# Two PSUM banks for the logits and three for the transposes, in place of three and two

## The chip, the cores and the metric

The kernel runs on one core of a Trainium2 chip. The metric is the time of one execution on the device in microseconds (us), as the median over runs; smaller is better. All inputs and results are float32.

## The reference

One layer of a hybrid decoder for 1040 positions (16 learned meta tokens and 1024 real ones) of width 1024. The input is RMS-normalised and multiplied by one wide matrix, whose columns feed two branches:

```python
u = _rmsnorm(h, norm_g)
proj = einsum('bld,de->ble', u, w_in)
q, k, v, f_logit, z_attn, gate_b, gate_c, xc, z_conv = split(proj, ...)
cum_logf = cumsum(log_sigmoid(f_logit + b_f))
# attention, 8 heads of 64: logit[t, s] = q_t.k_s / 8 + c[t] - c[s], s <= t
attn = softmax(logit) @ v
y_attn = group_rmsnorm(attn) * silu(z_attn)
# short convolution of width 3 over positions, 512 channels
y_conv = group_rmsnorm(gate_b * conv3(gate_c * xc)) * silu(z_conv)
out = rmsnorm(h + concat(y_attn, y_conv) @ w_out)
```

## The kernel before, in words

Every float32 product is made of three passes of a reduced type: each operand is split into a high and a low part, and high x high, high x low and low x high are added up in PSUM. So nearly all of the work is matmuls of TensorE.

The program has three stages. The first (to about 147 us of the profiled span, with its last projection blocks running up to the first logits at 165.8) makes the normaliser, the projections for q, k, v and the forget gates, and writes them to DRAM. The third (from about 489.5 us) is the output projection and the last norm. The second, in between, is where the change lies: it weaves the attention of eight heads with the remaining 20 blocks of the input projection (L167; their results are gate, convolution and SiLU inputs).

The attention of a head works on eight blocks of 128 queries. Blocks 4 to 7 form the half c=1, blocks 0 to 3 the half c=0. For each half:
- `s_step` (L604 to L621) makes the logits of one query block against one stretch of keys (144 to 456 columns, table SCH): two matmuls into a PSUM tile pn (L612, L613), on VectorE the maximum of each row (L616 with the causal mask on the block's last stretch, L619 on the others), on ScalarE the exponential into SBUF with the row sums (L620, two instructions in the profile: the exponential, and the read of the sums). The half c=1 has nine such steps in a head and c=0 has five, 112 in all.
- `s_end` (L623 to L643) joins the stretches: small operations on VectorE, GpSimd and ScalarE, then GpSimd multiplies every stretch of the probabilities by its factor (L642).
- `t_step` (L645 to L670) transposes the probabilities for one block of 128 keys: up to four transposes on TensorE into one PSUM tile pt (L660), a corner on VectorE for the diagonal (L664, L665), then ScalarE copies the high part out (L668) and VectorE subtracts it to get the low part pl (a helper at L117). There are 96 such tiles.
- `v_step` (L672 to L680) multiplies them with v into the PSUM tile po (L679), and `fold` reads po out.

PSUM has eight banks, and each of these tiles is one. In the second stage the pools divide them so: pj two (projection blocks and the group norms), psn three (the tiles pn), pst two (the tiles pt), pso one (po). A pool hands its banks out in turn; the first matmul into a tile waits until the last reader of the tile that had the bank before has ended. For pn this is the second of ScalarE's instructions at L620, for pt VectorE's subtraction.

What sets the order: on TensorE it is written out by hand. The steps of all heads are laid out by places (S_AT, T_AT, V_END, V_LAG) at L725 to L755; `weave` (L757 to L772) puts matmuls of the projection between them by a running account of work; and `pinned` (L108) keeps these TensorE instructions in program order. Logits of the next half run while the present half is transposed and multiplied. The order of VectorE, ScalarE and GpSimd isn't fixed by hand: a planner that walks the program with its own estimates of durations sets it when the kernel is built (L916). The DMA queue of SyncE loads the next head's q, k and v and the weight blocks.

After the second stage the pools psn, pst and pso are closed, and their six banks serve the output projection (five accumulators p, L783, and one for a norm, L784); `ring` (L844) opens seven cells, two of them in pj.

Of the kernel before, what the change touches and what calls it, by code (L numbers as in the profile page):

```python
# [14 lines left out]
PSUM = bass.MemoryType.PSUM  # L15
# [20 lines left out]
def hybrid_kernel(ctx, tc, hT, h, w_q, w_vf, w_m, w_o, gn, bf, cw, ga, gc, gf, out):  # L36
# [352 lines left out]
    own = ctx.enter_context(tc.tile_pool(name="own", bufs=1, reuse_waits="tile"))  # L389
    cp = ExitStack()  # L390
    pj = ctx.enter_context(tc.tile_pool(name="pj", bufs=2, space=PSUM, reuse_waits="tile"))
    psn = cp.enter_context(tc.tile_pool(name="psn", bufs=3, space=PSUM, reuse_waits="tile"))
    pst = cp.enter_context(tc.tile_pool(name="pst", bufs=2, space=PSUM, reuse_waits="tile"))
    pso = cp.enter_context(tc.tile_pool(name="pso", bufs=1, space=PSUM, reuse_waits="tile"))
    stk = ctx.enter_context(tc.tile_pool(name="stk", bufs=2, reuse_waits="tile"))
    pnp = cp.enter_context(tc.tile_pool(name="pnp", bufs=1, reuse_waits="tile"))
# [398 lines left out]
    def out_mm(n, es):  # L795
        t, c0, w = cells[n]
        tt, cs = slice(t * P, t * P + P), slice(c0, c0 + w)
        for e in es:
            for i, (a, b) in enumerate(((mhi[e], whi[e]), (mhi[e], wlo[e]), (mlo[e], whi[e]))):
                ins = nc.tensor.matmul(held[n][:, :w], a[:, tt], b[:, cs], start=(e == ORDER[0] and i == 0),  # L800
                                       stop=(e == ORDER[-1] and i == 2))
                if n < AHEAD:
                    pinned(ins)
        return ins.ins.name
# [42 lines left out]
    for i, e in enumerate(ORDER):  # L847
# [7 lines left out]
        for k, n in enumerate(ring):  # L855
            name = out_mm(n, [e])
# [63 lines left out]
```

## Time and profile before

| what | value |
|---|---|
| median of 3 runs | 587.3 us (586.95 to 587.99) |
| the profiled execution's own time | 588.21 us |
| its span, from the first to the last instruction | 585.9 us |
| TensorE matmuls / weight loads, busy | 574.7 us / 509.5 us |
| VectorE, ScalarE, GpSimd, busy | 376.1, 293.5, 135.5 us |
| first and last logit step (L612) | at 165.8 and 467.3 us |
| first and last transposes (L660) | at 182.2 and 482.2 us |

The engines are PE (TensorE's matmuls), PEld (its weight loads, which run beside the matmuls), DVE (VectorE), ACT (ScalarE), POOL (GpSimd) and SP (SyncE). Times in a timeline are microseconds from the start of the span; L612 is line 612 of the kernel. The ends of matmuls are modelled, and they overlap in the rows, so what tells of TensorE is when one starts and how long it sat idle. In brackets behind an instruction stands the idle time of its engine just before it and what ended it; "issue" there means that the profile shows nothing that it waited for.

### The profile page before, as it was taken

The page shows a single profiled execution, that of the slowest core. Times are in us where ns is not written, and L with a number is a line of the kernel's source. Part 1 is how long each engine was busy: PE and PEld are TensorE (multiplying, and loading weights), DVE is VectorE, ACT ScalarE, POOL GpSimd, SP SyncE. Part 2 cuts the span into 40 slices and gives each one's busy share as a digit, 9 for nine tenths or more (in the row PEclk, how much of TensorE's full clock was granted, in tenths as well). Part 3 has the DMA queues.
Part 4 walks back from the last instruction along what each step waited for, and adds up shares of the span by engine and source line. Part 5 has one row for each costly group of instructions (what it writes and reads, how often), then busy time and mean ns, then how long its engine had stood idle before and what let it go on. Part 6 is the DMA issues. An engine that isn't in the chain of part 4 may idle for free.

```text
span 585.9 us, 9143 instructions
## 1 busy us (share of the span) xinstructions
PE 574.7 (98%) x3230; PEld 509.5 (87%) x3230; DVE 376.1 (64%) x850; ACT 293.5 (50%) x679; POOL 135.5 (23%) x280
## 2 busy tenths in 40 slices
PE   9999999999999999999989999999999999999995
PEld 6889999999998889988879988888998878888884
DVE  5515852133377676897776897786788778747342
ACT  5355431131055575566763665756656568715231
POOL 1102011121105344144053153440540420000000
PEclk9999999999999999999999999999999999999999
DMA  8764594239417614416126126142251046643201
GB/s 295 220 208 143 190 361 136 80 114 293 148 36 186 146 37 134 124 58 153 49 77 146 58 74 164 63 121 75 80 212 37 4 160 227 240 162 131 86 36 72
DMA packets 35222, 78.14 MB, mean 133 GB/s; under 512 B 4025, under 2 KB 13385, under 8 KB 35177
## 3 DMA queue, kind: packets, MB, share of 16 engines
q1 hardware_dynamic: 35032, 77.57, 42.8%
q8 instruction: 25, 0.41, 0.3%
q14 instruction: 21, 0.16, 0.1%
q10 hardware_dynamic: 144, 0.00, 0.0%
HBM read 55.92 MB, written 21.64 MB: 132 GB/s over the span
## 4 chain that ended last, share of the span: by engine, by line
PE 50%; DVE 3%; POOL 2%; issue 0%; ACT 0%; POOLq 0%; ACTq 0%
PE pj L167 22%; PE p L800 10%; PE pj L800 5%; PE po L679 4%; PE pt L660 4%; PE pn L612 2%; PE pn L613 2%; POOL pn L642 1%; PE pj L414 0%; PE pj L415 0%; DVE gy L419 0%; DVE pn L616 0%; DVE pl L117 0%; DVE gy L418 0%; DVE wmlo L117 0%
## 5 line engine op out<-in xcount | busy, mean ns | idle before, releaser
L167 PE MATMUL pj<-xhi,wmhi 128*128 128x512 f32 (+1 forms) x384 | 144.8, 377 | 0.1
L167 PE MATMUL pj<-xhi,wmlo 128*128 128x512 f32 (+1 forms) x384 | 137.2, 357 | 0.0
L167 PE MATMUL pj<-xlo,wmhi 128*128 128x512 f32 (+1 forms) x384 | 136.7, 356 | 0.0
L167 PEld LDWEIGHTS pj<-xhi,wmlo 128*128 128x128 f32 x384 | 72.1, 188 | 8.3
L167 PEld LDWEIGHTS pj<-xhi,wmhi 128*128 128x128 f32 x384 | 72.6, 189 | 5.1 <-DVE cx L453 0.8
L167 PEld LDWEIGHTS pj<-xlo,wmhi 128*128 128x128 f32 x384 | 72.8, 190 | 3.8
L620 ACT ACTIVATE pn<-pn,nmx 128x328 f32<-128x328 f32 (+6 forms) x112 | 60.6, 542 | 30.7 <-DVE nmx L616 20.8
L642 POOL TENSOR_SCALAR pn<-pn,fc 128x328 f32<-128x328 f32 (+4 forms) x112 | 69.0, 637 | 1.6
L668 ACT CAST ph<-pt 128x512 fp32r<-128x512 f32 (+1 forms) x96 | 46.9, 490 | 39.7 <-DVE pt L665 16.4
L117 DVE TENSOR_TENSOR pl<-pt,ph 128x512 fp32r<-128x512 f32 (+1 forms) x96 | 54.7, 571 | 15.1 <-ACT ph L668 13.4
L114 POOL TENSOR_SCALAR wmhi<-wm 128x1024 fp32r<-128x1024 f32 x24 | 25.8, 1074 | 153.9 <-PE pj L167 85.5
L660 PE MATMUL pt<-ident,pn 128*128 128x128 f32 x288 | 47.3, 273 | 2.8 <-POOL pn L642 1.6
L660 PEld LDWEIGHTS pt<-ident,pn 128*128 128x128 f32 x288 | 36.2, 140 | 12.6 <-POOL pn L642 3.5
L616 DVE CUSTOM_DVE_ANT_0 pn<-pn,maskn 128x328 f32<-128x328 f32 (+3 forms) x64 | 31.9, 500 | 11.9 <-PE pn L613 11.2
L117 DVE TENSOR_TENSOR wmlo<-wm,wmhi 128x1024 fp32r<-128x1024 f32 x24 | 29.3, 1221 | 11.3 <-POOL wmhi L114 11.2
L612 PE MATMUL pn<-k,q 128*128 128x328 f32 (+6 forms) x112 | 36.5, 327 | 0.0
L613 PE MATMUL pn<-k,q 66*128 66x328 f32 (+6 forms) x112 | 36.1, 323 | 0.0
L679 PE MATMUL po<-ph,v 128*128 128x512 f32 (+1 forms) x96 | 33.8, 353 | 0.0
L679 PE MATMUL po<-pl,v 128*128 128x512 f32 (+1 forms) x96 | 33.6, 353 | 0.0
L167 PE MATMUL ps<-xhi,wmhi 128*128 128x346 f32 (+1 forms) x96 | 30.9, 322 | 0.0
L167 PE MATMUL ps<-xlo,wmhi 128*128 128x346 f32 (+1 forms) x96 | 30.8, 321 | 0.0
L619 DVE TENSOR_REDUCE nmx<-pn 128x1 f32<-128x346 f32 (+4 forms) x48 | 25.0, 523 | 9.1 <-PE pn L613 8.9
(232 smaller groups left out, 1209.6 us busy)
## 6 DMA issues: line engine op xcount, KB each, us to landing
wm<-in_w_m SPq DMA_DIRECT2D x24, 512.0 KB, 4.1
k<-kd SPq DMA_DIRECT2D x24, 260.0 KB, 5.9
q<-qd SPq DMA_DIRECT2D x24, 256.0 KB, 5.2
vd<-vv SPq DMA_DIRECT2D x9, 512.0 KB, 2.9
v<-vd SPq DMA_DIRECT2D x8, 576.0 KB, 6.4
ht<-in_h SPq DMA_DIRECT2D x8, 512.0 KB, 6.4
yd<-gy SPq DMA_DIRECT2D x16, 256.0 KB, 2.0
q<-in_w_o SPq DMA_DIRECT2D x8, 512.0 KB, 4.8
```

Source lines behind the costliest of these rows:

```text
L114: nc.gpsimd.tensor_scalar(hi, src, 1.0, 1.0, ALU.mult, ALU.mult)
L117: nc.vector.tensor_tensor(lo, src, f(hi), ALU.subtract)
L167: ins = nc.tensor.matmul(ps[:, :w], wt[:, k, :], xt[:, t0:t0 + w], start=(k == 0 and n == 0), stop=(k == KT - 1 and n == 2))
L612: pinned(nc.tensor.matmul(ps[:, :w], q1[:, qs], k1[:, ks], start=True, stop=False))
L613: pinned(nc.tensor.matmul(ps[:, :w], q2[:DH + 2, qs], k2[:DH + 2, ks], start=False, stop=True))
L616: nc.vector.tensor_tensor_reduce(ps[:, :w], ps[:, :w], maskn[:, MASKW - w:], op0=ALU.add, op1=ALU.min, scale=-1.0, scalar=-NEG, accum_out= ...
L620: nc.scalar.activation(pn[j][:, ks], ps[:, :w], AF.Exp, bias=nmx[c][at], scale=-1.0 if last else 1.0, accum_out=smx[c][at])
L642: nc.gpsimd.tensor_scalar(pn[j][:, k0:k0 + w], pn[j][:, k0:k0 + w], fc[:, j % 4, i:i + 1], 1.0, ALU.mult, ALU.mult)
L660: pinned(nc.tensor.transpose(pt[:, q0:q0 + P], pn[j][:, ks], ident))
L668: nc.scalar.copy(ph[:, at:], pt[:, at:])
L679: pinned(nc.tensor.matmul(po[:, at:], v2[:, vk, :], t if vk == 8 else t[:, at:], start=(kt == 0 and i == 0), stop=(kt == 4 * c + 4 and i = ...
L800: ins = nc.tensor.matmul(held[n][:, :w], a[:, tt], b[:, cs], start=(e == ORDER[0] and i == 0), stop=(e == ORDER[-1] and i == 2))
```

## The change

One bank goes from the pool of the logit tiles pn to the pool of the transposed tiles pt. Nothing else is edited.

```diff
-    psn = cp.enter_context(tc.tile_pool(name="psn", bufs=3, space=PSUM, reuse_waits="tile"))
-    pst = cp.enter_context(tc.tile_pool(name="pst", bufs=2, space=PSUM, reuse_waits="tile"))
+    psn = cp.enter_context(tc.tile_pool(name="psn", bufs=2, space=PSUM, reuse_waits="tile"))
+    pst = cp.enter_context(tc.tile_pool(name="pst", bufs=3, space=PSUM, reuse_waits="tile"))
```

## Rows read from the trace of the kernel before

**Rows 1.** The page, parts 1 and 2: busy time by engine; granted clock in 40 slices.

```profile
PE 574.7 (98%) x3230; PEld 509.5 (87%) x3230; DVE 376.1 (64%) x850; ACT 293.5 (50%) x679; POOL 135.5 (23%) x280
PEclk9999999999999999999999999999999999999999
```

**Rows 2.** Who waited for whom, whole span: us in total, times, longest.

```profile
PEld pt L660 <- POOL pn L642: 3.5, 5, 2.0
...
PE pt L660 <- POOL pn L642: 1.6, 1, 1.6
...
PE pt L660 <- DVE pl L117: 0.9, 1, 0.9
```

**Rows 3.** Timeline, 441 to 445.2 us: start, us, engine and line; logit steps and reads.

```profile
441.76 0.34 PE L612 MATMUL pn<-k,q 128*128 128x392 f32 x1
...
442.30 0.19 ACT L620 ACTIVATION_READ_ACCUMULATOR pn<-pn,nmx 128x1 f32 x1
...
443.95 0.34 PE L612 MATMUL pn<-k,q 128*128 128x392 f32 x1
...
444.42 0.20 ACT L620 ACTIVATION_READ_ACCUMULATOR pn<-pn,nmx 128x1 f32 x1
...
445.00 0.37 PE L612 MATMUL pn<-k,q 128*128 128x456 f32 x1
```

**Rows 4.** The tile pn, whole span: count, ns least/median/most, first and last start.

```profile
L613 PE MATMUL pn<-k,q x112: 274/322/377, 166.0 to 467.4; 66*128 66x328 f32 x16, 66*128 66x392 f32 x16, 66*128 66x456 f32 x16, 66*128 66x346 f32 x16
L620 ACT ACTIVATE pn<-pn,nmx x112: 362/550/643, 166.9 to 469.2; 128x328 f32<-128x328 f32 x16, 128x392 f32<-128x392 f32 x16, 128x456 f32<-128x456 f32 x16, 128x346 f32<-128x346 f32 x16
L620 ACT ACTIVATION_READ_ACCUMULATOR pn<-pn,nmx x112: 189/193/217, 167.4 to 469.5; 128x1 f32 x112
...
L616 DVE CUSTOM_DVE_ANT_0 pn<-pn,maskn x64: 302/514/642, 167.2 to 468.3; 128x328 f32<-128x328 f32 x8, 128x392 f32<-128x392 f32 x8, 128x456 f32<-128x456 f32 x8, 128x348 f32<-128x348 f32 x8
L619 DVE TENSOR_REDUCE nmx<-pn x48: 417/513/633, 166.3 to 466.0; 128x1 f32<-128x346 f32 x16, 128x1 f32<-128x328 f32 x8, 128x1 f32<-128x392 f32 x8, 128x1 f32<-128x456 f32 x8
```

**Rows 5.** Busy us by stretch: PE, PEld, DVE, ACT, POOL, then granted clock, DMA share.

```profile
441.00:452.00 11.00, 11.00 (x58) 9.43 (x57) 9.23 (x24) 8.22 (x25) 0.00 (x0) 1.00 0.16 49
343.00:347.00 4.00, 2.95 (x21) 2.41 (x20) 3.87 (x11) 2.19 (x6) 0.45 (x1) 1.00 0.17 66
```

**Rows 6.** Timeline: loads of four transposed tiles, one tile's matmuls, and a read before them.

```profile
343.73 0.42 PEld L660 LDWEIGHTS pt<-ident,pn 128*128 128x128 f32 x4 [0.39 <-POOL pn L642]
...
345.40 0.69 DVE L117 TENSOR_TENSOR pl<-pt,ph 128x512 fp32r<-128x512 f32 x1
...
346.21 0.42 PEld L660 LDWEIGHTS pt<-ident,pn 128*128 128x128 f32 x4 [1.16 <-issue]
...
346.24 0.63 PE L660 MATMUL pt<-ident,pn 128*128 128x128 f32 x4 [0.90 <-DVE pl L117]
...
384.23 0.42 PEld L660 LDWEIGHTS pt<-ident,pn 128*128 128x128 f32 x4 [0.45 <-PE pj L167]
...
482.18 0.14 PEld L660 LDWEIGHTS pt<-ident,pn 128*128 128x128 f32 x1 [0.42 <-PE pj L414]
```

**Rows 7.** Timeline: the first and the last late pair of logit step and read.

```profile
169.52 0.37 PE L612 MATMUL pn<-k,q 128*128 128x456 f32 x1
169.57 0.19 ACT L620 ACTIVATION_READ_ACCUMULATOR pn<-pn,nmx 128x1 f32 x1
...
450.30 0.32 PE L612 MATMUL pn<-k,q 128*128 128x348 f32 x1
450.30 0.20 ACT L620 ACTIVATION_READ_ACCUMULATOR pn<-pn,nmx 128x1 f32 x1
```

**Rows 8.** The tile pt, its last reader; and the chain, first output matmuls (start, us).

```profile
L117 DVE TENSOR_TENSOR pl<-pt,ph x96: 296/633/692, 183.8 to 485.0; 128x512 fp32r<-128x512 f32 x48, 128x416 fp32r<-128x416 f32 x16, 128x288 fp32r<-128x288 f32 x16, 128x160 fp32r<-128x160 f32 x16
...
489.51 3.45 PE p L800 x15
```

## The prediction

> **What bounds the kernel.** I read the page's busy times first: TensorE is busy 98% of a 585.9 us span, VectorE 64%, ScalarE 50%, and the granted clock is at its upper level (2.4 GHz) in every slice [rows 1]. Busy time of TensorE overstates, since the matmuls overlap, so I then read what TensorE and its weight loads waited for. There is very little: in the whole span the matmuls wait 1.6 us once for GpSimd's normalising of the probabilities, 0.9 us once for VectorE's reading of a transposed tile, and the weight loads 3.5 us in five places for GpSimd [rows 2]. TensorE's order in the woven stage is written out by hand, and it takes its instructions strictly in that order; so any microsecond for which one of them waits for a bank is a microsecond on everything behind it, the projection's matmuls included, up to the output projection, which is TensorE's own work to the end. What counts is therefore only this: which matmuls have to wait for a bank before, and which after.
>
> What is *not* in the list of waits is the first finding: not one of the 112 logit steps (L612) waits for its bank with three banks. The closest is the step that starts at 445.00: the step three before it was read out at 444.42 + 0.20 = 444.62, 0.38 us earlier [rows 3].
>
> **How long a logit bank is held.** A bank is taken by the first matmul (L612) and given back when ScalarE's second instruction (the read of the row sums) ends. At its shortest that is about 0.15 us to the second matmul, then, by the medians, 0.32 for it, 0.51 for VectorE's maximum, 0.55 for the exponential and 0.19 for the read: 1.7 us [rows 4]. Taken step by step from the trace (end of the read minus start of L612) the shortest are 1.70 for 346 columns and 2.07 for 400; the median is 2.1 and the longest 4.3, because VectorE and ScalarE have other work in front. With two banks a step waits for the one two before it. The steps come in eight bursts of nine (query blocks 4 to 7 of a head), with five sparse ones between. In the last burst VectorE is busy 9.2 and ScalarE 8.2 of 11 us [rows 5], and nine steps start between 440.37 and 450.30, 1.24 us apart on average. Two spacings, 2.5 us, are about what a hold takes: enough on average, too short where two steps are put close together.
>
> **The cost of the bank taken away.** A wait before the matmuls of a full bank ends 0.15 us after the reader's end: the transposes at 346.24 follow a read that ended at 345.40 + 0.69 = 346.09 [rows 6]. So a step is late by (end of the read two steps before) + 0.15 - (its own start). In the last burst: the step at 441.76 needs the read that ends at 442.30 + 0.19 = 442.49, so it waits 0.88. The next, at 443.95, would be late by 444.62 + 0.15 - 443.95 = 0.82, but it has itself been moved 0.88 later by the first wait, so if the read keeps its time it no longer waits; nor does the one at 445.00 [rows 3]. Two more pairs, the first and the last in the kernel: the step at 169.52 needs the read that ends at 169.76, late by 0.39; that at 450.30 one that ends at 450.50, late by 0.35 [rows 7]. Over the 110 steps done this way 23 are late, the first and the last of them these two:
> - Added up as they stand, with every later hold shifted too: 11.5 us. That is the upper end.
> - If all holds were at the shortest for their width, so that VectorE and ScalarE use every wait to catch up: eight waits, 2.7 us. That is the lower end.
> - Between: inside a burst a read keeps its traced time unless its own step was moved past it (then the shortest hold counts), and each burst starts afresh, because both engines' work hangs on TensorE's results and moves with them. By burst: 0.67, 1.03, 1.09, 0.68, 0.07, 1.04, 1.03, 0.88, in all 6.5 us in 16 steps.
>
> I take 6.5: between bursts the traced queues show the other engines filled again, which speaks against the lower end, and inside one each wait lets them empty, which speaks against the upper.
>
> **The gain of the bank added.** A transposed tile is held from its transposes to the end of VectorE's pl (L117), which reads it last. With two banks four of the 96 tiles start 0.15 us after the release they need, the sign of a wait: those whose loads start at 343.73, 346.21, 384.23 and 482.18, after the load queue had been idle for 0.39, 1.16, 0.45 and 0.42 us, 2.4 in all [rows 6]. (One of them the view puts down to GpSimd.) Of that the profile counts only 0.9 as idle time of the matmuls [rows 2]. Bounds 0.9 and 2.4; I take the middle, 1.7. With three banks every one of the 96 has its bank free at least 1.6 us early, so no such wait is left. A third bank gives no more than that: the transposes can't be issued earlier than their place in TensorE's order.
>
> **What costs nothing.** The number of instructions on every engine, their shapes and the transfers stay as they are. The output projection lays its five accumulators over the same six banks; with two logit banks its third cell falls on a former transpose bank. The last read of one starts at 485.0 and the output matmuls start at 489.51 [rows 8], a cover of 4 us. The order of VectorE's, ScalarE's and GpSimd's instructions isn't written by hand: a planner at build time sets it with its own estimates, and may shift it when the bank counts change; that is a risk in both directions, priced among the rivals.
>
> **The sum.** 6.5 - 1.7 = +4.8 us. The profiled execution took 588.21 us (its span 585.9 and 2.3 around it), 0.9 above the median of 587.3; the sum is a difference, so it goes on the median: 592.1. What is late next is the last step of a burst, so GpSimd's normalising behind it shifts with the bursts and its waits [rows 2] stay.
>
> **The rivals.**
> 1. *The waits are absorbed.* After the first waits VectorE and ScalarE run ahead for good, and holds fall to the shortest: 2.7 - 1.7 = +1.0, 588.3. For it: ScalarE has half of its time free. Against: in the bursts it is busy three quarters of the time, VectorE more [rows 5].
> 2. *Faster.* The place is the bursts, the mechanism the planner: seeing only two banks, it puts the maximum and the exponential of a step ahead of the conversions queued before them, so that holds fall to 1.7 us and, where two steps stand close, the conversions wait instead. From the point where the logit waits come to less than the gain of 1.7 the kernel is faster; with 0.5 us of waits left it is 1.2 faster, 586.1, with none 585.6. Against: even with the shortest holds eight steps stay late, by 2.7 us, because their starts are too close.
> 3. *All add up.* The engines don't catch up, or the planner's new order lengthens the holds: 11.5 less the lower gain of 0.9, +10.6, 597.9. For it: holds up to 4.3 us occur now.
> 4. *The clock falls.* Now TensorE's granted clock is 1.00 in the last burst, and also in the 4 us that hold the idle 1.16 us [rows 5, 6]. If new short waits made it fall to its lower level (1.2 GHz) in the bursts, which last 82 us together, they would take twice as long: about +87, 674. The rows speak against it: short waits already occur and the clock holds through them. The Trainium skill (TensorE: Matmul & The Clock Gate, section "A second HAM failure mode: psum-queue depth-cycling") tells of a kernel that cycled through banks and idled so often between groups that its clock went back and forth; by that rule this rival would come about, and the trace of before doesn't agree, since 1.00 stands across its bank waits.
>
> Another page bears on the direction. The Trainium skill (Perfetto Trace Analysis, "Optimization Strategy") says that a gap which keeps coming back on the engine that should be full can mean too few buffers; by it the four gaps at the transposes call for the third bank, which is the 1.7 us above. It says nothing of the pool that gives the bank up.
>
> **How the numbers follow.** Forecast 0.60; rival 1 0.15; rival 2 0.08; rival 3 0.15; rival 4 0.02. A measurement of this kernel can tell about 0.2%, 1.2 us, from no change. Faster by more than that: rival 2, 0.08. Within: rival 1 and the lowest edge of the forecast, 0.17. Slower: 0.75. The range goes from 587.2 (2.7 of waits against 2.4 of gain is +0.3, 587.6, and a little below it for the run-to-run spread) to 598.5 (just above rival 3); left out are rival 2, rival 4 and the outer parts of 1 and 3, about 0.2.
>
> **What would show it.** In the changed profile L612 should appear in the waits of TensorE and its loads, released by ScalarE's L620, some 15 to 25 times, 3 to 11 us in all, mostly in the eight bursts and none in the sparse steps between; L660 should wait for GpSimd alone; the granted clock should stay 1.00; the output projection should take the time that it takes now and just start later. The prediction is wrong if L612 waits are absent or below 2 us, if TensorE's loss lies at other lines (L167, L679: another order on VectorE), or if the clock row shows dips.

## The result and the profile after

The changed kernel takes 593.61 us (median, 592.7 to 594.33) against 587.64 us for the kernel before in the same series: 6.0 us more, a ratio of 1.0088 with a 95% interval of 1.0062 to 1.0115. A later series (E10) gave 593.82 against 587.99, 1.0088 (1.0070 to 1.0106). The profiled execution of the changed kernel spans 591.9 us, 6.0 more than the 585.9 of before.

The page of the changed kernel, parts 1 and 2, beside [rows 1]:

```profile
span 591.9 us, 9141 instructions
...
PE 577.4 (98%) x3230; PEld 508.3 (86%) x3230; DVE 377.4 (64%) x850; ACT 293.2 (50%) x679; POOL 134.1 (23%) x280
...
PEclk9999999999999999999999999999999999999999
```

Same instruction counts, nearly the same busy times, the same clock. By busy shares nothing happened; TensorE is "98% busy" in both. Where the time went is in what TensorE waited for. The list of waits of the changed kernel, beside [rows 2] (us in total, times, longest):

```profile
PE pn L612 <- ACT pn L620: 4.3, 10, 0.8
...
PE pt L660 <- POOL pn L642: 0.8, 1, 0.8
PE pj L167 <- DVE cx L453: 0.4, 1, 0.4
...
PEld pn L612 <- ACT pn L620: 10.0, 17, 1.2
...
PEld pt L660 <- POOL pn L642: 1.2, 1, 1.2
```

A wait has appeared that the kernel before did not have: the logit step (L612) for ScalarE's second instruction at L620, 17 times at the weight loads, 10 of them long enough to show at the matmuls as well. The wait of the transposes for VectorE's L117 is gone, and their wait for GpSimd has halved. One projection matmul (L167) now waits 0.4 us for VectorE's L453; that one has to do with the order of VectorE, not with the banks, as E3 shows below.

One such wait, in the last burst of nine steps; the timeline of the changed kernel, beside [rows 3]:

```profile
446.03 0.31 PE L612 MATMUL pn<-k,q 128*128 128x328 f32 x1
446.18 0.31 PE L613 MATMUL pn<-k,q 66*128 66x328 f32 x1
...
446.87 0.19 ACT L620 ACTIVATION_READ_ACCUMULATOR pn<-pn,nmx 128x1 f32 x1
447.12 0.19 PEld L612 LDWEIGHTS pn<-k,q 128*128 128x128 f32 x1 [0.90 <-ACT pn L620]
447.12 0.45 PE L612 MATMUL pn<-k,q 128*128 128x392 f32 x1 [0.63 <-ACT pn L620]
447.22 0.19 PEld L613 LDWEIGHTS pn<-k,q 66*128 66x128 f32 x1
447.40 0.34 PE L613 MATMUL pn<-k,q 66*128 66x392 f32 x1
...
448.42 0.19 ACT L620 ACTIVATION_READ_ACCUMULATOR pn<-pn,nmx 128x1 f32 x1
...
449.42 0.34 PE L612 MATMUL pn<-k,q 128*128 128x392 f32 x1
449.42 0.19 PEld L613 LDWEIGHTS pn<-k,q 66*128 66x128 f32 x1
```

This is the step that the prediction worked out (441.76 before). The read that it needs ends at 446.87 + 0.19 = 447.06; the step starts some 0.05 us later. Its second matmul comes 0.28 us after the first; the same step in the kernel before, as wide, took 0.18 (441.76 to 441.94). The load of its second weights begins 0.10 us behind the first matmul (447.22 against 447.12); in the next step, which doesn't wait, the two begin together (449.42). The next step, at 449.42, no longer waits, as expected: the read of its bank ended at 448.61.

To add the waits up I used that TensorE's matmuls come in the same order in all three traces: for each matmul of the second stage I took the time from the start of the one ahead of it to its own, less the same distance in the kernel before. The table sums these differences by the two lines, in us.

| place | changed | old order (E2) |
|---|---|---|
| start of L612 (behind L167 or another step) | +6.8 | +8.1 |
| L613 behind its L612 | +2.0 | +1.9 |
| the matmul behind L613 | +0.5 | 0.0 |
| start of the transposes, L660, with the rest of the stage | -2.7 | -1.7 |
| all places in the stage | +6.5 | +8.4 |

The +0.5 behind L613 lies at a single matmul, the one of L167 that waits for L453.

The stages tell the same. The second stage, from the first logit step to the first output matmul, lasted 489.3 - 165.8 = 323.5 us before. The line of L800 before, and then the lines of L612 and L800 in the changed kernel:

```profile
L800 PE MATMUL p<-whi,mhi x77: 279/389/397, 489.3 to 578.4; 128*128 128x512 f32 x70, 128*128 128x256 f32 x7
```

```profile
L612 PE MATMUL pn<-k,q x112: 230/333/477, 165.3 to 473.3; 128*128 128x328 f32 x16, 128*128 128x392 f32 x16, 128*128 128x456 f32 x16, 128*128 128x346 f32 x16
...
L800 PE MATMUL p<-whi,mhi x77: 279/389/398, 495.3 to 584.4; 128*128 128x512 f32 x70, 128*128 128x256 f32 x7
```

(the two times are the first and last start), so 330.0 us, 6.5 more. From the first output matmul to the end it is 96.6 us in both.

### The profile page after: what moved, and what is told of

Its sections match the earlier page's. It is cut to its first block, busy times and chain, and to the rows that moved or that the text cites. A ratio compares the mean times of both kernels' runs of the same rounds, so it can differ in the third digit from the quotient of the medians.

```text
span 591.9 us, 9141 instructions
## 1 busy us (share of the span) xinstructions
PE 577.4 (98%) x3230; PEld 508.3 (86%) x3230; DVE 377.4 (64%) x850; ACT 293.2 (50%) x679; POOL 134.1 (23%) x280
## 4 chain that ended last, share of the span: by engine, by line
PE 82%; DVE 7%; ACT 5%; POOL 2%; issue 1%; DMA 1%; POOLq 0%; SPq 0%; ACTq 0%; DVEq 0%
PE pj L167 29%; PE p L800 10%; PE ps L326 8%; PE ps L167 8%; PE ps L234 7%; PE pj L800 5%; PE po L679 5%; PE pt L660 4%; PE pn L612 3%; ACT pn L620 2%; PE pn L613 2%; DVE pl L117 1%; POOL pn L642 1%; PE px L234 1%; DVE wmlo L117 1%
## 5 line engine op out<-in xcount | busy, mean ns | idle before, releaser
L167 PE MATMUL pj<-xhi,wmhi 128*128 128x512 f32 (+1 forms) x384 | 145.0, 378 | 0.6 <-DVE cx L453 0.4
L167 PE MATMUL pj<-xhi,wmlo 128*128 128x512 f32 (+1 forms) x384 | 137.1, 357 | 0.0
L167 PE MATMUL pj<-xlo,wmhi 128*128 128x512 f32 (+1 forms) x384 | 136.7, 356 | 0.0
L620 ACT ACTIVATE pn<-pn,nmx 128x328 f32<-128x328 f32 (+6 forms) x112 | 60.5, 541 | 38.0 <-DVE nmx L616 25.4
L167 PEld LDWEIGHTS pj<-xhi,wmlo 128*128 128x128 f32 x384 | 72.2, 188 | 8.3
L167 PEld LDWEIGHTS pj<-xhi,wmhi 128*128 128x128 f32 x384 | 72.6, 189 | 6.0 <-DVE cx L453 1.3
L167 PEld LDWEIGHTS pj<-xlo,wmhi 128*128 128x128 f32 x384 | 72.8, 189 | 3.8
L642 POOL TENSOR_SCALAR pn<-pn,fc 128x328 f32<-128x328 f32 (+4 forms) x112 | 68.0, 628 | 1.6
L117 DVE TENSOR_TENSOR pl<-pt,ph 128x512 fp32r<-128x512 f32 (+1 forms) x96 | 54.7, 571 | 16.8 <-ACT ph L668 15.4
L660 PE MATMUL pt<-ident,pn 128*128 128x128 f32 x288 | 47.1, 272 | 0.8 <-POOL pn L642 0.8
L660 PEld LDWEIGHTS pt<-ident,pn 128*128 128x128 f32 x288 | 36.7, 140 | 8.9 <-POOL pn L642 1.2
L612 PE MATMUL pn<-k,q 128*128 128x328 f32 (+6 forms) x112 | 38.5, 345 | 4.6 <-ACT pn L620 4.3
L613 PE MATMUL pn<-k,q 66*128 66x328 f32 (+6 forms) x112 | 36.1, 322 | 0.0
L117 DVE TENSOR_TENSOR wmlo<-wm,wmhi 128x1024 fp32r<-128x1024 f32 x24 | 29.3, 1220 | 10.5 <-POOL wmhi L114 10.4
L612 PEld LDWEIGHTS pn<-k,q 128*128 128x128 f32 x112 | 21.1, 188 | 12.6 <-ACT pn L620 10.0
L167 PE MATMUL ps<-xhi,wmhi 128*128 128x346 f32 (+1 forms) x96 | 31.0, 323 | 0.0
```

What stands on the lines that cost most here:

```text
L117: nc.vector.tensor_tensor(lo, src, f(hi), ALU.subtract)
L167: ins = nc.tensor.matmul(ps[:, :w], wt[:, k, :], xt[:, t0:t0 + w], start=(k == 0 and n == 0), stop=(k == KT - 1 and n == 2))
L612: pinned(nc.tensor.matmul(ps[:, :w], q1[:, qs], k1[:, ks], start=True, stop=False))
L613: pinned(nc.tensor.matmul(ps[:, :w], q2[:DH + 2, qs], k2[:DH + 2, ks], start=False, stop=True))
L620: nc.scalar.activation(pn[j][:, ks], ps[:, :w], AF.Exp, bias=nmx[c][at], scale=-1.0 if last else 1.0, accum_out=smx[c][at])
L642: nc.gpsimd.tensor_scalar(pn[j][:, k0:k0 + w], pn[j][:, k0:k0 + w], fc[:, j % 4, i:i + 1], 1.0, ALU.mult, ALU.mult)
```

## The experiments

Each had the kernel before beside it on the same chip. The first four ran together, so did the next four, and the last three. The second stage is read from one profiled execution of each; two such executions of one kernel gave 330.0 and 329.4 (changed, E10), and 321.8 twice (E4, E11).

| run | banks, logits + transposes | median us | before us | ratio (95%) | second stage, us |
|---|---|---|---|---|---|
| before | 3 + 2 | | 587.64 | | 323.5 |
| changed | 2 + 3 | 593.61 | 587.64 | 1.0088 (1.0062 to 1.0115) | 330.0 |
| E1 | 2 + 2, one bank unused | 602.69 | 588.58 | 1.0242 (1.0221 to 1.0264) | 332.6 |
| E2 | 2 + 3, order of before | 595.75 | 588.58 | 1.0137 (1.0108 to 1.0165) | 331.9 |
| E3 | 3 + 2, order of the changed | 588.55 | 588.58 | 1.0006 (0.9987 to 1.0025) | 324.6 |
| E4 | one pool of 5 | 587.62 | 588.58 | 0.9975 (0.9957 to 0.9992) | 321.8 |
| E5 | 2 + 2, eighth bank held in place | 596.57 | 587.98 | 1.0137 (1.0116 to 1.0158) | 331.3 |
| E6 | one pool of 5, earlier bursts | 590.20 | 587.98 | 1.0036 (1.0015 to 1.0057) | 325.9 |
| E7 | 2 + 3, no row sums | 593.18 | 587.98 | 1.0081 (1.0055 to 1.0108) | 328.1 |
| E8 | 3 + 2, no row sums | 591.18 | 587.98 | 1.0040 (1.0024 to 1.0055) | 325.0 |
| E9 | 1 + 3, one held unused | 665.73 | 587.99 | 1.1302 (1.1264 to 1.1340) | 403.1 |
| E10 | 2 + 3, the changed again | 593.82 | 587.99 | 1.0088 (1.0070 to 1.0106) | 329.4 |
| E11 | one pool of 5, again | 586.41 | 587.99 | 0.9969 (0.9953 to 0.9985) | 321.8 |

**E1: only the logit bank is taken.** The order of the other four engines' instructions is held to that of before (the edit is shown at E2).

```diff
-    psn = cp.enter_context(tc.tile_pool(name="psn", bufs=3, space=PSUM, reuse_waits="tile"))
+    psn = cp.enter_context(tc.tile_pool(name="psn", bufs=2, space=PSUM, reuse_waits="tile"))
```

> Two logit banks and two transpose banks, one bank unused; VectorE, ScalarE, GpSimd and SyncE held to the order of the kernel before. My theory (bank waits alone): the logit steps pay what they paid in the changed kernel, by the starts of its matmuls 9.3 us (6.8 at L612, 2.5 just behind it), and the transposes keep their own waits: about 8 to 9 us over the kernel before, 596, so 2 to 3 us slower than the changed kernel, with about 17 waits of L612 for L620. Rival (the third transpose bank gives nothing): as the changed kernel, +6.0, 593.6. Rival (the planner's new order costs the time, not the banks): with the old order held, within 1.5 us of the kernel before.

It was 14 us slower, outside every expectation. The waits of E1:

```profile
PE pn L612 <- ACT pn L620: 4.6, 11, 0.8
PE p L800 <- DVE o L691: 3.8, 1, 3.8
PE pt L660 <- POOL pn L642: 1.6, 1, 1.6
...
PE pt L660 <- DVE pl L117: 0.9, 1, 0.9
```

The L612 waits are the expected ones, and the transposes wait as in [rows 2]. What was not foreseen is L800: with seven banks in use, one of the output projection's five accumulators came to lie on the bank of po, and TensorE stood still until the last head was read out (L691). It cost more than its 3.8 us: from the first output matmul to the end E1 takes 102.2 us, against 96.6 before. Busy time by stretch (PE, PEld, DVE, ACT, POOL, then the granted clock):

```profile
498.00:505.00 7.00, 3.23 (x14) 2.29 (x13) 6.28 (x8) 4.81 (x7) 0.00 (x0) 0.99 0.91 331
...
505.00:508.50 3.50, 3.50 (x10) 2.81 (x9) 2.59 (x3) 3.09 (x5) 0.00 (x0) 0.53 0.85 281
```

After that idle stretch the granted clock fell to its lower level (0.5, 1.2 GHz) for some 3 us, with 10 output matmuls in 3.5 us. So E1's total does not isolate the bank; E5's does. E1's second stage, which was over before that wait, does: 332.6 us, 9.1 more than before, as expected of the logit steps.

**E2 and E3: banks against order.** The diff says nothing of order, but the planner did set another one: the changed kernel has TensorE's sequence unaltered and VectorE's and ScalarE's shuffled in places. At the end of the kernel function each engine's instructions are tied, in the order of the other kernel, each behind its predecessor (an edge for the order of issue, not a wait; the lists ORDERS of instruction names are left out here):

```diff
+    by = {i.name: i for i in tc.nc.cur_bb.bb.instructions}
+    for names in ORDERS:
+        chain = [n for n in ("I-" + x for x in names.split(",")) if n in by]
+        for a, b in zip(chain, chain[1:]):
+            tc.add_manual_dep(by[b], a, mybir.DependencyInfo(
+                mybir.DependencyClass.NoSync, mybir.DependencyReason.SCHED_ONLY), reason="order")
```

> The changed kernel's banks (two and three) with the kernel before's order of VectorE, ScalarE, GpSimd and SyncE. My theory: the banks set the time, the order nothing: +5 to +7 us over the kernel before, 593 to 594.5, with 15 to 25 waits at L612. Rival (order): +0 to +1.5 us. In between, the difference to +6.0 is the order's share.

> The kernel before's banks (three and two) with the changed kernel's order of VectorE, ScalarE, GpSimd and SyncE. My theory: within 1.2 us of the kernel before, no wait at L612. Rival (order): +4 to +6 us, and the loss shows at lines other than L612.

E3 is the kernel before within the interval (about 1.1 us to either side), without one wait at L612. Its second stage is 1.1 us longer in the profile, with none of it at L612 and 0.5 at the matmul of L167 that waits for L453: the new order by itself costs about 1 of the 6 us at most. E2 is 7.2 us slower by the medians, a little over the expected 5 to 7, with 17 waits at L612's loads:

```profile
PE pn L612 <- ACT pn L620: 5.4, 12, 0.8
PE pt L660 <- POOL pn L642: 1.6, 1, 1.6
...
PEld pn L612 <- ACT pn L620: 11.3, 17, 1.2
PEld pt L660 <- POOL pn L642: 3.0, 4, 2.1
```

So the banks are the cause. The planner's new order softens it: with it the second stage is 1.9 us shorter (330.0 against 331.9), 1.3 at L612 and 1.0 at L660, where the longest wait of the loads for GpSimd falls from 2.1 us to 1.2, less the 0.5 at L167.

E1 and E2 differ in the third transpose bank alone, and have one order. E2's stage is shorter by only 0.7 us (331.9 against 332.6): the transposes start 1.6 us less late, but one logit step behind them, at 366.77 us, waits 0.8 more. The wait of that step varies: in the two profiled executions of the changed kernel (changed, E10) it differs by 0.6. So whether a part of the gain comes back at the logit steps isn't shown.

**E4 and E11: one pool of five for both kinds.**

```diff
-    psn = cp.enter_context(tc.tile_pool(name="psn", bufs=3, space=PSUM, reuse_waits="tile"))
-    pst = cp.enter_context(tc.tile_pool(name="pst", bufs=2, space=PSUM, reuse_waits="tile"))
+    psn = cp.enter_context(tc.tile_pool(name="psn", bufs=5, space=PSUM, reuse_waits="tile"))
...
-        ps = psn.tile([P, 512], F32, name="pn")
+        ps = psn.tile([P, 512], F32, name="pt")
...
-        pt = pst.tile([P, 512], F32, name="pt")
+        pt = psn.tile([P, 512], F32, name="pt")
```

> Logit and transposed tiles take their banks from one pool of five in turn, in place of three and two apart. My theory: by the trace of before no tile then finds its bank held (each needs the fifth-last tile of either kind to be read out, and all 208 are early), so the four waits of the transposes go and none comes at L612: 1 to 2 us faster than before, 585.6 to 586.6. Rival (a tile that is held long, up to 5 us for a transposed one, stands in the way of logit steps): waits of 2 us or more at L612, 589 or more. Rival (the transposes then wait for GpSimd instead): within 0.8 us of before.

> The one pool of five banks once more on the same chip: 1 to 2 us below before, 7 below the changed kernel, no wait of L611 (the logit step's first matmul there) and none of the transposes for L117.

Waits of TensorE in E4 (the logit steps are L611 here, the transposes L659; of the matmuls the list has two more lines, 1.3 us at L206 and 0.2 at L167):

```profile
PE pt L659 <- POOL pn L641: 1.6, 1, 1.6
...
PE ps L234 <- DVE wqhi L221: 0.3, 1, 0.3
...
PEld pt L659 <- POOL pn L641: 3.0, 4, 2.0
```

No logit step and no transpose waits for a bank; the waits for GpSimd are those of before. The second stage is 1.7 us shorter than before in both profiles, which is the gain that the prediction gave the third transpose bank, here without its price. It isn't the order: in the trace VectorE and ScalarE work in the order of before but for 4 of 850 and 2 of 679 places. The medians are 1.0 and 1.6 us below before, both with intervals that exclude equality: this version beats both kernels. Its two profiled executions took 585.61 and 590.47 us with the same second stage of 321.8: in E11's the first logit step came at 170.2 instead of 165.3, after a 2.4 us wait in the first stage, behind which the granted clock was 0.50 from 52.9 to 56.3 us:

```profile
PE ps L167 <- ACT qraw L242: 2.4, 1, 2.4
```

**E5: the logit bank alone, mended.** A pool that is written once holds the eighth bank between the two:

```diff
+    spare = cp.enter_context(tc.tile_pool(name="spare", bufs=1, space=PSUM, reuse_waits="tile"))
+    nc.vector.memset(spare.tile([P, 512], F32, name="spare"), 0.0)
```

> Again two logit and two transpose banks, but the eighth bank is now held, unused, by a pool between them (one memset of it on VectorE), so that the output projection finds the banks that it had before: in the first such run one of its accumulators fell on the bank of po and waited 4 us. My theory: the L612 waits stay (about 17, 9 us with what follows them) and the four waits of the transposes come back, the wait at L800 goes: 8 to 10 us over before, 2 to 3 us more than the changed kernel. Rival (the third transpose bank is worth the whole 7 us between the first and the second run): 13 to 15 us over before.

As expected, +8.6 us. Its waits (L614 is the logit step, L662 the transposes):

```profile
PE pn L614 <- ACT pn L622: 4.1, 10, 0.8
...
PE pt L662 <- DVE pl L117: 0.9, 2, 0.6
...
PEld pn L614 <- ACT pn L622: 9.5, 16, 1.2
```

The logit waits are those of the changed kernel, the waits of the transposes for L117 are back, and L800 waits no more. VectorE and ScalarE work in the order of the changed kernel but for 4 and 2 places, so the two differ in the third transpose bank alone. Against the changed kernel (+6.0) it is worth 2.6 us by the medians and 1.3 by the stage lengths (1.9 against E10's). E5's profiled execution was late before the second stage, with its first logit step at 167.2 instead of 165.3 us, so a part of the 2.6 may have nothing to do with the bank.

**E6: more room, denser bursts.** One pool of five, and

```diff
-    S_AT = ((0.0, 0.5), (0.0, 0.425), (0.0, 0.37))
+    S_AT = ((0.0, 0.5), (0.0, 0.39), (0.0, 0.37))
```

> One pool of five banks, and the nine logit steps of the half c=1 laid out over the first 0.39 of their stage in place of 0.425, 0.8 us earlier at the end. What is left of waits in the one-pool kernel is L660 for GpSimd (1.6 us at one tile, 3.0 at the weight loads). Theory: GpSimd's normalising starts earlier, these waits fall by 0.8 us in each of the heads where they occur, and five banks bear the denser steps: 1 to 2 us faster than the one-pool kernel, 2 to 3.5 us faster than before. Rival: denser steps run into the banks or into a full VectorE, L612 or L167 waits come up: no faster than the one-pool kernel or slower.

A miss: slower than before, and the wait that it was to shorten got longer. The waits, and the busy time around the longest, which ended at 263.0 us (PE, PEld, DVE, ACT, POOL, then the granted clock):

```profile
PE pt L659 <- POOL pn L641: 3.1, 2, 2.3
```

```profile
260.00:263.70 3.70, 1.39 (x9) 0.92 (x8) 3.64 (x7) 2.05 (x6) 3.70 (x5) 1.00 0.62 218
263.70:267.20 3.50, 3.50 (x12) 2.86 (x12) 2.73 (x4) 1.17 (x2) 3.05 (x5) 0.51 0.19 74
```

Five banks bore the denser steps (no wait at the logit steps), but GpSimd did not finish sooner against the transposes. Behind the wait of 2.3 us the granted clock fell to its lower level for 3.4 us, which at half the pace is another 1.7 us or so (an estimate). The six of the 12 runs with a mean clock of 0.995 or less took 590.7 to 594.2 us, the six others 588.3 to 589.7, so a part of this miss goes with the clock. Why GpSimd finished no sooner stays open; TensorE's order changes with this edit, so it isn't a clean comparison.

**E7 and E8: a shorter hold.** The exponential without its row sums, so the read at L620 goes; the sums are set to 1.

```diff
-        nc.gpsimd.memset(smx[c], 0.0)
+        nc.gpsimd.memset(smx[c], 1.0)
...
-        nc.scalar.activation(pn[j][:, ks], ps[:, :w], AF.Exp, bias=nmx[c][at], scale=-1.0 if last else 1.0,
-                             accum_out=smx[c][at])
+        nc.scalar.activation(pn[j][:, ks], ps[:, :w], AF.Exp, bias=nmx[c][at], scale=-1.0 if last else 1.0)
```

> The changed kernel's banks, and the exponential without its row sums: ScalarE's second instruction at L620 (0.19 us) goes, and with it the normalising by the sums is left out (they are set to 1). Theory: what costs is how long a bank is held, so with every hold 0.19 us shorter the same rule over the trace of before gives 4.5 us of waits in 13 steps instead of 6.5 in 16, less if ScalarE's queue also empties: 2 to 4 us faster than the changed kernel, +2 to +4 over before. Rival (the rate at which VectorE and TensorE get through the bursts, not the hold): +5 to +6, no change.

> The same without row sums (normalising by them left out) on the kernel before, three and two banks. Theory: no logit step waited for its bank there, so a shorter hold gives nothing: within 1 us of before. Rival (22 us less work of ScalarE is worth something by itself): 1.5 us faster or more, and that has to be taken off the run with two and three.

The waits of E7, and then of E8:

```profile
PE pn L612 <- ACT pn L620: 3.0, 8, 0.7
...
PEld pn L612 <- ACT pn L620: 7.4, 13, 1.1
```

```profile
PE pt L659 <- POOL pn L641: 3.4, 2, 2.3
...
PE pt L659 <- DVE pl L117: 0.9, 1, 0.9
```

At the place in question the theory held: 13 steps wait instead of 17, and the excess at L612 is 5.0 us instead of 6.8; the rule over the trace of before had given 13 and 4.5. The total did not come out: E7 is at +5.2 and not +2 to +4, and E8, which should have been as before, is 3.2 us slower, with twice the wait for GpSimd and runs from 588.8 to 592.1. The planner's order changes when the instructions do, and the second stage of E8's profiled execution is only 1.5 us longer. That execution was the fastest of the 12, with a mean granted clock of 0.999; the seven runs at 0.995 or less have a median of 591.6 us, the five others 589.7. So a part of E8's loss goes with the clock, and where in the kernel no trace here shows. Set against each other, E7 and E8 are 2.0 us apart by the medians and 3.1 by the stage, where the kernels with row sums are 6.0 and 6.5 apart. This fits the hold as the cost. The edit also takes the reads, 22 us of ScalarE's work, away, and a shorter hold by itself isn't told apart from a shorter queue before it.

**E9: one logit bank.**

```diff
-    psn = cp.enter_context(tc.tile_pool(name="psn", bufs=2, space=PSUM, reuse_waits="tile"))
+    psn = cp.enter_context(tc.tile_pool(name="psn", bufs=1, space=PSUM, reuse_waits="tile"))
```

(from the changed kernel, with the spare bank of E5).

> One logit bank, a bank held unused in its neighbourhood, three transpose banks: every logit step now waits for the one before it. My theory (a step waits until the read of the tile that had its bank ends, plus 0.15 us, and the second matmul behind a wait comes 0.10 us later): by the rule on the trace of before, burst by burst, 55 us in 62 steps, 6 us behind them, 1.7 to 2.7 off for the transposes: +55 to +62 over before, 643 to 650. Rival (VectorE and ScalarE run ahead in the waits, so the price levels off): +30 or less. Rival (the clock falls with so many waits): over +75, and the granted clock below 0.97.

It is 77.7 us slower. The waits, and the clock of one stretch with the first logit steps and of one between bursts:

```profile
PE pn L614 <- ACT pn L622: 48.9, 56, 2.0
...
PEld pn L614 <- ACT pn L622: 71.4, 65, 2.3
```

```profile
165.00:175.00 10.00, 6.81 (x33) 5.46 (x32) 5.72 (x14) 3.19 (x9) 0.00 (x0) 0.86 0.00 1
246.00:258.00 12.00, 12.00 (x77) 11.49 (x76) 7.69 (x22) 4.67 (x12) 5.30 (x11) 1.00 0.77 185
```

The total misses my +55 to +62. By starts the steps wait 60 us, in 65 places (expected 55 in 62), and 9 us come behind them (expected 6). So the rule comes near at ten times the waits, though the planner set yet another order here, and the starts include what the clock added. The rest is the rival that I had named: in the first of these stretches TensorE idles 3.2 of 10 us, and in the stage its granted clock falls to the lower level ten times, for some 41 us together (0.966 on average over the span), and matmuls at L167, which waited for nothing, take 10 us longer.

**E10: the changed kernel again.**

> The changed kernel once more, beside the one-pool kernel on the same chip: +6 us over before (5 to 7), 18 waits of L612.

+5.8 us, 17 waits at the loads (9.3 us); 7.4 us above the one pool of five (E11).

## Why the prediction was right, step by step

- *The direction and its mechanism.* Shown. Forecast was 592.1 us, +4.8; it was 593.6, +6.0, inside the range. The logit steps wait for a bank, released by L620, 17 times, in the bursts alone; the output projection starts 6 us later and takes as long as before; the clock stays up in the second stage. E2 and E3 rule out the order of the other engines as the cause.
- *The cost of the bank taken away*, 6.5 us, was too small: 8.8 in the changed kernel (L612 and L613), 10.0 with the order of before (E2). A term was missing: a step that waits has the load of its second weights late too, so L613 comes 0.10 us later, 2.0 us in 19 steps (by their starts; the list of waits names 17). And the rule inside a burst let the reads keep their traced times; with the same order the waits at L612 were 8.1 us, between the middle value and the upper end, so the reads kept less to their times than I took. The 0.15 us from a release to the start, taken from the transposes, was wrong for this place: it is 0.05, and with 0.05 the same rule gives only 5.5 us, in 13 steps. So that slip hid a part of the other error.
- *The gain of the bank added*, 1.7 us, is right for what it named: with the order of before the four named tiles start 0.3, 1.1, 0.2 and 0.2 us less late (E2), and E4's second stage is 1.7 shorter. In the changed kernel the transposes gain 2.7, because under the planner's new order they also wait less for GpSimd, at 302.58 us 0.8 less; E3 has this too, and I had said that these waits stay. Beside two logit banks the stage is shorter by 0.7 (E1 to E2), 1.3 (E5 to the changed kernel) or 1.9 us (E5 to E10) with the third transpose bank; these differ mostly by the wait of the one logit step near 366 us. The sum took gain and cost as independent, and whether they are stays open.
- *The sum.* +4.8 came close partly by luck: both terms were too small, the cost by 2.3 and the gain by 1.0, and the planner's order added 0.5 at L167.
- *What was costed at nothing.* Instruction counts and the output projection: right. The planner's order: within 1.1 us of nothing for the kernel before (E3); in the changed one its stage is 1.9 us shorter by it (E2), and the medians are 1.2 apart, which is less than the intervals allow for.
- *Rival 1*, absorbed waits: out, the waits came to more than the forecast. *Rival 2*, faster by a better order: the planner did set another order, and 1.3 us less is waited at L612 with it, far from what the rival needed. *Rival 3*: out at 11.5, but nearer to E2's 8.1 at L612 than rival 1's 2.7. *Rival 4*, the clock: out for the change, where the longest wait is 1.2 us and the clock stays at 1.00; in E9, with 65 waits of up to 2.3 us, it comes true beside the waits. The Trainium skill (TensorE: Matmul & The Clock Gate, "A second HAM failure mode: psum-queue depth-cycling") tells of a kernel whose clock went back and forth because it idled so often between groups of matmuls; E9 agrees, with ten falls, and the changed kernel, with its 17 waits, does not.
- *The other page.* The Trainium skill's rule of the returning gap (Perfetto Trace Analysis, "Optimization Strategy") found the right shortage, four gaps at the transposes; E4 shows that it could be met without making another.

## What to carry to other kernels

Before moving a buffer from one pool to another, list for each use of the poorer pool when its buffer of n uses ago was given back; where that is later than the use itself, the difference is a wait of an engine that works in a fixed order, and the sum of those is an upper bound of the price (11.5 us here, where 8.1 was waited with the same order), since a first wait moves the later uses too. An average spacing that fits says little: the waits come from pairs that stand closer than the average. When two pools are short at different times, one pool for both can serve where neither split does (E4, E11). An experiment that leaves a bank unused must see to it that later pools still get the banks that they had (E1, E5).

## What was not expected of the hardware

- After a wait at the first of two matmuls with different weights, the second comes 0.10 us later than usual, though it waits for nothing: 0.28 instead of 0.18 us behind it.
- The start of a matmul after the release that it waited for came at one of two distances, whichever engine released it: about 0.05 us (the logit steps after ScalarE's read, the transposes after GpSimd's L642, L167 after VectorE's L453) or about 0.15 (the transposes after VectorE's subtraction, L800 after VectorE's L691 in E1, L167 after ScalarE's L242 in E5). What decides between them no run here shows.
- One idle stretch of 4.2 us of the weight loads (3.8 of the matmuls) in E1 was followed by matmuls at the lower clock (0.53 granted from 505.0 to 508.5 us), and so were waits of the matmuls of 2.3 us in E6 (0.51 from 263.7 to 267.2) and of 2.4 us in E11. One of 2.3 us in E8 left it at 1.00, as did the waits of up to 1.2 us, seventeen of them, in the changed kernel.
